# One step of a hybrid recurrent decoder on one core: sample-row outputs and the S5 input matrix on four column groups, modulation in 512-column matmuls

## The chip, the core and the metric

The kernel runs on one core of one Trainium2 chip. The metric is the device time of one execution in microseconds (us); the time of a kernel is the median of its runs.

## What is computed

Two layers of a decoder trunk of width 1024 act on a prompt (512 tokens) and on eight sample rows (one token each, with recurrent states of their own). Per layer:

```python
mod = silu(c) @ w_ada[l] + b_ada[l]            # (9 rows, 6 x 1024): shift, scale, gate, twice
h   = x * (1 + sc_m) + sh_m
out = mixer(h)                                 # layer 0: GLA and RG-LRU; layer 1: S5 and HGRN2
x   = layer_norm(ALPHA * x + (1 + gt_m) * out)
h   = x * (1 + sc_f) + sh_f
x   = layer_norm(ALPHA * x + (1 + gt_f) * swiglu(h, ffn_w_in[l], ffn_w_out[l]))
# GLA and HGRN2, each sample row b and head h, one token:
S[b,h] = diag(a[b,h]) S[b,h] + k[b,h]^T v[b,h]   # (64 x 128 in GLA, 128 x 128 in HGRN2)
o[b,h] = q[b,h] S[b,h]                           # one row of 128
# S5, each of 32 groups g: the response matrix of an 8-token block is made of C_g A_g^e B_g, e = 0..7
```

All arrays are float32. `c` holds nine rows: one for the prompt, eight for the samples.

## The kernel before, in words

Activations lie with features on the 128 partitions and tokens along the free dimension, in two halves of 260 columns (256 prompt tokens and 4 sample rows). A projection is done in units of 128 output features. Each unit splits its weights into a high and a low float32r part (ScalarE casts at L199, VectorE subtracts through the helper at L110) and runs three matmuls per 128 inputs and half: high times high (L237), high times low (L239), low times high (L241). The first units behind a layer norm run one half after the other (L816 to L818). These matmuls of 260 columns are most of TensorE's work.

All weights come through one stream: the list `plan` fixes the order of the pieces, mostly 1 MB each, `WS.load` (L176) issues their loads on SyncE's queue into three buffers, and `WS.take` hands them out in the same order. The pieces of the modulation weights `w_ada` stand in that list between the projections' pieces, placed by `mix`. `WS.ada`, called before and after a unit, takes the modulation pieces that are next. The order of instructions on each engine is chosen when the program is made, by a scheduler that keeps its own estimate of when each operand is ready and otherwise follows the order of the program.

Three places matter here.

- **Modulation.** The first two of layer 0's six parts are made at the start (`ada_mm`, L312). The other ten parts of 1024 columns are made from 40 pieces, four for a part: a piece is 256 rows by 1024 columns of `w_ada`. `ada_part` (L323) runs 8 matmuls for it, two of 128 rows for each of four column groups of the array, with the 32-column `condT` as the stationary operand and 256 columns of weights moving. After the fourth piece `ada_rows` copies the result (ScalarE, L328), turns it with two transposes (L147) and adds the bias on VectorE. The plan places 12 pieces in layer 0's mixer, 8 and 8 in the two halves of its FFN, 8 in layer 1's input projection and 4 at the start of layer 1's FFN.
- **Sample rows.** `la_samples` goes in steps of four rows and one group of heads: 4 steps in GLA (two heads of 64 rows each on the partitions, `hpt` = 2), 8 in HGRN2 (`hpt` = 1). A step makes the outer products with one matmul (L1066, 32 or 64 rows of the array), updates four states on VectorE (L122), multiplies each by its query (L1073: the 128x128 state is the stationary operand, one or two query columns move), copies the result (L1074) and stores the states.
- **S5 input matrix.** `s5_prep` works through four chunks of 8 groups inside layer 0's FFN. Each chunk transposes `BA`, and then multiplies each group's 128x128 `BA` (stationary) by 16 columns of `CS` (L1620), and copies the 128 columns to `Mall` (L1622).

A float32 matmul stands in the trace as two instructions (passes), a float32r matmul as one.

Of the kernel before, what the change touches and what calls it, by code (L numbers as in the profile page):

```python
# [16 lines left out]
D = 1024  # L17
# [22 lines left out]
def build(tc, I, O):  # L40
    nc = tc.nc
    V, S, G, T, SY = nc.vector, nc.scalar, nc.gpsimd, nc.tensor, nc.sync
    with ExitStack() as ctx:
# [65 lines left out]
        def tt(out, a, b, op):  # L109
            V.tensor_tensor(out=out, in0=a, in1=b, op=op)  # L110
# [41 lines left out]
        class WS:  # L152
# [60 lines left out]
            def ada(self):  # L213
                while self.i < len(units) and plan[units[self.i][0]][0] == "ada":
                    p_, _, r = self.take()
                    if p_[2] == 0:
                        self.acc = mx()
                    ada_part(self.acc, p_[2], r)
                    if p_[2] == 6:
                        ada_rows(self.acc, p_[6], p_[4] // 128)  # L220

            def get(self, kind, c0, k0=0, j=0):
# [23 lines left out]
        f_out = [I["ffn_w_out"][l] for l in range(2)]  # L246

        def p_ada(l, js):
            return [("ada", I["w_ada"][l], k0, 2, D * j, D, l) for j in js for k0 in range(0, 8, 2)]

        def p_cols(kind, src, cols):
            return [(kind, src, 0, 8, c, 256) for c in cols]
# [13 lines left out]
        def mix(main, ada, first=1, per=2):  # L266
            r = list(main[:first])
            rest = main[first:]
            done = 0
            for n, c in enumerate(rest):  # L270
                want = (n + 1) * (len(ada) // per) // len(rest) * per
                r += ada[done:want]
                done = want
                r.append(c)
            return r

        FA = p_ada(0, [5]) + p_ada(1, [0])
        FB = p_ada(1, [1, 2])
        OA = p_ada(1, [3, 4])
        LA = p_ada(1, [5])  # L280
        plan.append(("lr", ev_in, 0, 8, 1536, 16))
        plan += p_cols("in", ev_in, [0])
        plan += mix(p_cols("in", ev_in, EV_COLS), p_ada(0, range(2, 4)))
        plan += mix(p_cols("out", ev_out, (0, 256)), p_ada(0, [4])[:2], 1) + p_ada(0, [4])[2:] + p_cols("out", ev_out, (512, 768))
        plan += mix(p_ffn(0, 0)[:12], FA[:4], 3) + mix(p_ffn(0, 0)[12:], FA[4:])
        plan += mix(p_ffn(0, 1)[:-4], FB, 2) + p_ffn(0, 1)[-4:]
        plan += mix(p_cols("in", od_in, OD_COLS), OA, 0, 1)
        plan.append(("glu", I["od_s5_w_glu"][0], 0, 4, 0, 512))
        plan += p_cols("out", od_out, range(0, D, 256))
        plan += mix(p_ffn(1, 0)[:12], LA, 2, 1) + p_ffn(1, 0)[12:] + p_ffn(1, 1)  # L290

        for n, p in enumerate(plan):
            for jj in range(1 if p[0] == "ada" else max(1, p[5] // 128)):
# [15 lines left out]
        def ada_mm(p, r):  # L309
            for k in range(8):  # L310
                c = k % 4
                T.matmul(p[32 * c:32 * c + 32, 0:256], condT[:, k, :], r[:, k, :],  # L312
                         start=(k < 4), stop=(k >= 4), tile_position=(0, 32 * c), skip_group_check=True)
            sb = cst.tile([128, 256], F32, tag="adasb", name="adasb")
            S.copy(sb, p[:, 0:256])
            for b in range(2):
                T.matmul(p[:, 256 + 16 * b:256 + 16 * b + 9], sb[:, 128 * b:128 * b + 128], sel, start=True, stop=True)
            return p[:, 256:288].rearrange("p (c r) -> p c r", r=16)[:, :, 0:9]

        def ada_part(p, k0, r):  # L320
            for k in range(2):
                for c in range(4):
                    T.matmul(p[32 * c:32 * c + 32, 0:256], condT[:, k0 + k, :], r[:, k, 256 * c:256 * c + 256],  # L323
                             start=(k0 + k == 0), stop=(k0 + k == 7), tile_position=(0, 32 * c), skip_group_check=True)

        def ada_rows(p, l, j):
            sb = cst.tile([128, 256], F32, tag="adasb", name="adasb")
            S.copy(sb, p[:, 0:256])  # L328
            for b in range(2):
                transpose(p[:, 256 + 128 * b:384 + 128 * b], sb[:, 128 * b:128 * b + 128])  # L330
            tt(mod[l][:, j:j + 8, :].rearrange("p (c b) r -> p b c r", b=2),
               p[:, 256:512].rearrange("p (b c r) -> p b c r", b=2, r=32)[:, :, :, 0:9],
               bc(vA[:, 48 * l + j:48 * l + j + 8].rearrange("p (c b) -> p b c", b=2).unsqueeze(3), [128, 2, 4, 9]), ALU.add)

        def split(hi, lo, src):
            last["split"] = S.copy(hi, src)
# [678 lines left out]
        def la_samples(mp_, vds, nt, dk, q_s, k_s, a_s, v_s, s_in, s_out, res):  # L1015
# [42 lines left out]
            for bh in range(2):  # L1058
                vd = vds()
                tt(vd.bitcast(F32R), bc(vT.unsqueeze(1), [128, 4, 128]), bc(m8[:, 4 * bh:4 * bh + 4].unsqueeze(2), [128, 4, 128]), ALU.mult)  # L1060
                for t_ in range(nt):
# [376 lines left out]
        def s5_prep(sp):  # L1438
            if True:
# [160 lines left out]
                for ch in range(4):  # L1600
# [417 lines left out]
```

## Time and profile before

| | |
|---|---|
| median of 3 runs (1388.51 to 1391.63) | 1388.89 us |
| the profiled execution's own time | 1391.37 us |
| its span, first to last instruction | 1389.4 us |
| mean granted TensorE clock | 0.985 |
| matmuls busy, share of the span | 96% |
| VectorE, ScalarE, GpSimd busy | 55%, 36%, 14% |
| bytes moved by DMA | 185.53 MB, mean 134 GB/s |

A busy matmul row says that a matmul was in flight; matmuls overlap, so what one costs is read from the starts of the instructions around it, and not from its duration.

### The profile page before, as it was taken

Reading aid. Unit: us, or ns where it says so; the run is one execution under the profiler, and the core shown is the slowest. Engines: PE = TensorE matmul, PEld = TensorE weight load, DVE = VectorE, ACT = ScalarE, POOL = GpSimd, SP = SyncE. Lnnn points to the kernel's source line nnn. Section 1 sums busy time; section 2 is a strip of 40 time slices with the busy share of each in tenths; the row PEclk is TensorE's granted clock in tenths of the full one; section 3 lists DMA queues with packets and bytes.
Section 4 is the critical chain, followed back from the end, with each engine's and each line's share of the span. In section 5 each row is a group of like instructions: output and inputs, shape, how many; then the busy total and the mean of one; then the engine's idle time right before and its main releaser. Section 6 shows DMA issues by size and latency. Waiting matters only on the chain. (4 is left out here: it accounts for less than half of the span.)

```text
span 1389.4 us, 29467 instructions
## 1 busy us (share of the span) xinstructions
PE 1333.4 (96%) x12687; PEld 1267.0 (91%) x12687; DVE 764.9 (55%) x1726; ACT 498.2 (36%) x802; POOL 191.8 (14%) x215
## 2 busy tenths in 40 slices
PE   6998999989999999999998999999999999999996
PEld 4797988989998999999988999889899999999996
DVE  4677755687997233233592785566833233232365
ACT  3555536353232222222264123363533222222231
POOL 2200010340011200000170421013500000000013
PEclk9999999999999999999999999999999999999998
DMA  9643363413345842444458446432333323221211
GB/s 277 197 152 101 91 212 120 154 48 120 116 166 205 234 152 92 152 133 158 150 200 169 131 147 216 126 126 92 101 113 107 118 95 122 92 92 54 84 62 63
DMA packets 157628, 185.53 MB, mean 134 GB/s; under 512 B 18188, under 2 KB 137354, under 8 KB 157242
## 3 DMA queue, kind: packets, MB, share of 16 engines
q1 hardware_dynamic: 151514, 166.43, 38.7%
q0 software_dynamic: 5744, 17.08, 3.8%
q8 instruction: 100, 1.64, 0.5%
q14 instruction: 30, 0.25, 0.1%
q10 hardware_dynamic: 240, 0.13, 0.0%
HBM read 167.11 MB, written 15.36 MB: 131 GB/s over the span
## 5 line engine op out<-in xcount | busy, mean ns | idle before, releaser
L237 PE MATMUL acc<-hhi,whi 128*128 128x260 f32 x1936 | 398.8, 287 | 3.0 <-ACT whi L199 1.3
L199 ACT CAST whi<-raw 128x1024 fp32r<-128x1024 f32 (+2 forms) x198 | 187.7, 955 | 587.1 <-PE acc L239 428.1
L239 PE MATMUL acc<-hlo,whi 128*128 128x260 f32 x1936 | 396.2, 286 | 1.2 <-DVE hlo L110 1.2
L241 PE MATMUL acc<-hhi,wlo 128*128 128x260 f32 x1936 | 395.1, 285 | 0.0
L110 DVE TENSOR_TENSOR wlo<-raw,whi 128x1024 fp32r<-128x1024 f32 (+2 forms) x198 | 220.2, 1116 | 222.3 <-ACT whi L199 220.7
L237 PEld LDWEIGHTS acc<-hhi,whi 128*128 128x128 f32 x1936 | 300.5, 190 | 16.1 <-issue 5.9
L239 PEld LDWEIGHTS acc<-hlo,whi 128*128 128x128 f32 x1936 | 300.6, 190 | 4.4 <-DVE hlo L110 1.7
L241 PEld LDWEIGHTS acc<-hhi,wlo 128*128 128x128 f32 x1936 | 300.9, 190 | 2.3 <-issue 1.7
L239 PE MATMUL acc<-al,whi 128*128 128x260 f32 x576 | 116.0, 283 | 2.3 <-DVE al L110 2.3
L237 PE MATMUL acc<-ah,whi 128*128 128x260 f32 x576 | 116.4, 284 | 1.4 <-DVE x L122 0.8
L241 PE MATMUL acc<-ah,wlo 128*128 128x260 f32 x576 | 115.7, 283 | 0.0
L110 DVE TENSOR_TENSOR sg<-acc,sg 128x520 f32<-128x520 f32 (+1 forms) x48 | 31.0, 653 | 112.6 <-PE acc L241 108.1
L237 PEld LDWEIGHTS acc<-ah,whi 128*128 128x128 f32 x576 | 88.3, 188 | 4.8 <-ACT whi L199 2.3
L239 PEld LDWEIGHTS acc<-al,whi 128*128 128x128 f32 x576 | 88.6, 188 | 2.5 <-DVE al L110 2.5
L241 PEld LDWEIGHTS acc<-ah,wlo 128*128 128x128 f32 x576 | 88.6, 188 | 0.0
L524 POOL TENSOR_TENSOR s<-x 128x520 f32<-128x520 f32 x4 | 6.9, 1720 | 568.1 <-ACT whi L199 321.6
L110 DVE TENSOR_TENSOR smp<-acc,gt 128x8 f32<-128x8 f32 (+1 forms) x72 | 11.6, 161 | 119.0 <-PE acc L241 94.5
L816 PE MATMUL acc<-hhi,whi 128*128 128x260 f32 x208 | 59.2, 287 | 3.3 <-ACT hhi L774 3.3
L818 PE MATMUL acc<-hlo,whi 128*128 128x260 f32 x208 | 58.8, 289 | 3.3 <-DVE hlo L767 1.9
L817 PE MATMUL acc<-hhi,wlo 128*128 128x260 f32 x208 | 58.3, 282 | 0.0
L122 DVE SCALAR_TENSOR_TENSOR x<-acc,gt,x 128x512 f32<-128x512 f32 (+1 forms) x72 | 44.8, 622 | 0.0
L323 PE MATMUL mx<-raw,condT 128*32 128x256 f32 x640 | 44.2, 384 | 0.0
(592 smaller groups left out, 2017.5 us busy)
## 6 DMA issues: line engine op xcount, KB each, us to landing
raw<-in_w_ada_dram SPq DMA_DIRECT2D x40, 1024.0 KB, 6.1
raw<-in_ffn_w_in_dram SPq DMA_DIRECT2D x40, 1024.0 KB, 5.2
raw<-in_ffn_w_out_dram SPq DMA_DIRECT2D x16, 1024.0 KB, 5.3
raw<-in_ev_w_in_dram SPq DMA_DIRECT2D x10, 1024.0 KB, 9.4
raw<-in_od_w_in_dram SPq DMA_DIRECT2D x10, 1024.0 KB, 5.9
raw<-in_w_ada_dram SPq DMA_DIRECT2D x16, 512.0 KB, 7.3
raw<-in_ffn_w_out_dram SPq DMA_DIRECT2D x16, 384.0 KB, 3.1
raw<-in_ev_w_out_dram SPq DMA_DIRECT2D x4, 1024.0 KB, 5.3
```

The lines of the kernel that those rows point to most:

```text
L110: V.tensor_tensor(out=out, in0=a, in1=b, op=op)
L122: V.scalar_tensor_tensor(out=out, in0=a, scalar=s, in1=b, op0=op0, op1=op1)
L199: S.copy(hi[:, :nk, :m], rj)
L237: T.matmul(acc[:, hf, :HN], wh[:, k - koff, :], ah(k)[:, hf, :], start=st, stop=False)
L239: T.matmul(acc[:, hf, :HN], wh[:, k - koff, :], al(k)[:, hf, :], start=False, stop=False)
L241: T.matmul(acc[:, hf, :HN], wl[:, k - koff, :], ah(k)[:, hf, :], start=False, stop=sp)
L323: T.matmul(p[32 * c:32 * c + 32, 0:256], condT[:, k0 + k, :], r[:, k, 256 * c:256 * c + 256], start=(k0 + k == 0), stop=(k0 + k == 7), til ...
L524: G.tensor_tensor(out=lnt["s1"], in0=x[:, 0] if m == 1 else lnt["s1"], in1=x[:, m], op=ALU.add)
L816: T.matmul(out, wh[:, k, :], ah(k)[:, hf, :], start=n == 0, stop=False)
L817: T.matmul(out, wl[:, k, :], ah(k)[:, hf, :], start=False, stop=False)
L818: T.matmul(out, wh[:, k, :], al(k)[:, hf, :], start=False, stop=n == len(ks) - 1)
```

## The change

Three edits, and a new placement of the modulation pieces that follows from the third.

1. In `la_samples` the query becomes the stationary operand, broadcast over the 32 columns of one column group, and the state's 128 columns move. The four rows of a step go to the four column groups. The result, with a row on each group of 32 partitions, is copied by ScalarE and transposed, once for each head of the step.
2. In `s5_prep` two groups' `CS` (32 columns) become the stationary operand and `BA`'s 128 columns move; eight matmuls fill the four column groups twice. Each computes a neighbour's product too. The result is copied, transposed in two blocks, and the wanted halves are copied to `Mall` by two strided copies.
3. A modulation piece is now 128 rows by 2048 columns, and a column group takes 512 moving columns. Eight pieces make two parts. The result fills a whole PSUM bank, so the transposes (four, for two parts) go to a second one.

```diff
-                    if p_[2] == 6:
+                    if p_[2] == 7:
                         ada_rows(self.acc, p_[6], p_[4] // 128)
...
-            return [("ada", I["w_ada"][l], k0, 2, D * j, D, l) for j in js for k0 in range(0, 8, 2)]
+            return [("ada", I["w_ada"][l], k, 1, D * j, 2 * D, l) for j in js for k in range(8)]
...
-        FA = p_ada(0, [5]) + p_ada(1, [0])
-        FB = p_ada(1, [1, 2])
-        OA = p_ada(1, [3, 4])
-        LA = p_ada(1, [5])
+        E2, E4 = p_ada(0, [2]), p_ada(0, [4])
+        FA, FB, OA = p_ada(1, [0]), p_ada(1, [2]), p_ada(1, [4])
...
-        plan += mix(p_cols("in", ev_in, EV_COLS), p_ada(0, range(2, 4)))
-        plan += mix(p_cols("out", ev_out, (0, 256)), p_ada(0, [4])[:2], 1) + p_ada(0, [4])[2:] + p_cols("out", ev_out, (512, 768))
+        plan += mix(p_cols("in", ev_in, EV_COLS), E2 + E4[:4])
+        plan += mix(p_cols("out", ev_out, (0, 256)), E4[4:6], 1) + E4[6:] + p_cols("out", ev_out, (512, 768))
...
-        plan += mix(p_ffn(1, 0)[:12], LA, 2, 1) + p_ffn(1, 0)[12:] + p_ffn(1, 1)
+        plan += p_ffn(1, 0) + p_ffn(1, 1)
...
-        def ada_part(p, k0, r):
-            for k in range(2):
-                for c in range(4):
-                    T.matmul(p[32 * c:32 * c + 32, 0:256], condT[:, k0 + k, :], r[:, k, 256 * c:256 * c + 256],
-                             start=(k0 + k == 0), stop=(k0 + k == 7), tile_position=(0, 32 * c), skip_group_check=True)
+        def ada_part(p, k, r):
+            for c in range(4):
+                T.matmul(p[32 * c:32 * c + 32, 0:512], condT[:, k, :], r[:, 0, 512 * c:512 * c + 512],
+                         start=(k == 0), stop=(k == 7), tile_position=(0, 32 * c), skip_group_check=True)
 
         def ada_rows(p, l, j):
-            sb = cst.tile([128, 256], F32, tag="adasb", name="adasb")
-            S.copy(sb, p[:, 0:256])
-            for b in range(2):
-                transpose(p[:, 256 + 128 * b:384 + 128 * b], sb[:, 128 * b:128 * b + 128])
...
+            sb = tmp.tile([128, 512], F32, tag="t2k", name="adarow")
+            S.copy(sb, p)
+            q = mx()
+            for b in range(4):
+                transpose(q[:, 128 * b:128 * b + 128], sb[:, 128 * b:128 * b + 128])
...
-                    for b in range(4):
-                        T.matmul(po[:, b * hpt:b * hpt + hpt], s0[:, b], qm[:, t_, 4 * bh + b], start=True, stop=True)
-                    V.tensor_copy(o_s[:, t_ * hpt:(t_ + 1) * hpt, 4 * bh:4 * bh + 4], po[:, 0:4 * hpt].rearrange("p (b h) -> p h b", h=hpt))
+                    for hh in range(hpt):
+                        for b in range(4):
+                            T.matmul(po[32 * b:32 * b + 32, 128 * hh:128 * hh + 128], bc(qm[:, t_, 4 * bh + b, hh:hh + 1], [128, 32]),
+                                     s0[:, b], start=hh == 0, stop=True, tile_position=(0, 32 * b), skip_group_check=True)
+                    ot = mp_.tile([128, hpt * 128], F32, tag="ot", name="ot")
+                    S.copy(ot, po[:, 0:128 * hpt])
+                    for hh in range(hpt):
+                        transpose(po[:, 256 + 128 * hh:384 + 128 * hh], ot[:, 128 * hh:128 * hh + 128])
+                    V.tensor_copy(o_s[:, t_ * hpt:(t_ + 1) * hpt, 4 * bh:4 * bh + 4],
+                                  po[:, 256:256 + 128 * hpt].rearrange("p (h b n) -> p h b n", h=hpt, n=32)[:, :, :, 0])
...
-                        gg = 8 * ch + g
-                        T.matmul(pM[:, g * 16:(g + 1) * 16], BA[:, g].rearrange("p e h -> p (e h)"), CS[:, gg],
-                                 start=True, stop=True)
-                    S.copy(Mall[:, 128 * ch:128 * ch + 128], pM[:, 0:128])
+                        c, gg = g % 4, 8 * ch + g - g % 2
+                        T.matmul(pM[32 * c:32 * c + 32, 128 * (g // 4):128 * (g // 4) + 128],
+                                 CS[:, gg:gg + 2].rearrange("p a b -> p (a b)"), BA[:, g].rearrange("p e h -> p (e h)"),
+                                 start=g < 4, stop=True, tile_position=(0, 32 * c), skip_group_check=True)
+                    mt = tmp.tile([128, 256], F32, tag="t2k", name="mt")
+                    S.copy(mt, pM[:, 0:256])
+                    for q in range(2):
+                        transpose(pM[:, 256 + 128 * q:384 + 128 * q], mt[:, 128 * q:128 * q + 128])
...
+                    for b in range(2):
+                        S.copy(mv[:, :, b], pM[:, 256:512].rearrange("p (a b d h) -> p a b d h", b=2, d=2, h=16)[:, :, b, b])
```

With the new pieces the plan places 16 in layer 0's mixer (12 before), 8 and 8 in the halves of its FFN as before, 8 in layer 1's input projection as before, and none in layer 1's FFN (4 before). The pieces are still 1 MB, 40 in all.

## Rows read from the trace of the kernel before

**Rows 1.** The page's first part: busy time of each engine, its share of the span, and its instructions.
```profile
PE 1333.4 (96%) x12687; PEld 1267.0 (91%) x12687; DVE 764.9 (55%) x1726; ACT 498.2 (36%) x802; POOL 191.8 (14%) x215
```
**Rows 2.** Who TensorE waited for: total us, times, longest us. The longest of 27 lines, and one more that the text speaks of.
```profile
PE mx L1716 <- DMA u<-Usd: 5.9, 1, 5.9
...
PE mx L1224 <- issue: 2.8, 1, 2.8
```
**Rows 3.** Groups of TensorE's instructions, shapes kept apart (of L1073 the shape of HGRN2's steps): line, operation, output<-inputs, shapes, count | busy us, mean ns of one | idle before.
```profile
L323 PE MATMUL mx<-raw,condT 128*32 128x256 f32 x640 | 44.2, 384 | 0.0
L1073 PE MATMUL mx<-qm,s 128*128 128x1 f32 x64 | 9.0, 240 | 1.0 <-DVE s L122 0.8
L1620 PE MATMUL mx<-CS,BA 128*128 128x16 f32 x64 | 7.4, 257 | 0.0
```
**Rows 4.** TensorE's timeline around one chunk's S5 products: start us, us, line, shapes, count of merged instructions.
```profile
391.80 0.41 PE L239 MATMUL acc<-hlo,whi 128*128 128x260 f32 x2
392.05 1.85 PE L1620 MATMUL mx<-CS,BA 128*128 128x16 f32 x16
393.75 0.48 PE L241 MATMUL acc<-hhi,wlo 128*128 128x260 f32 x2
394.08 0.40 PE L237 MATMUL acc<-hhi,whi 128*128 128x260 f32 x2
```
**Rows 5.** The same view at the sample rows' products. L1073 stands in 28 runs for 12 steps; these are the first run (GLA) and the last step (HGRN2), which stands in two.
```profile
176.27 0.72 PE L1073 MATMUL mx<-qm,s 128*128 128x2 f32 x6
...
912.07 0.28 PE L241 MATMUL acc<-y5h,wlo 128*128 128x260 f32 x1
912.18 0.50 PE L1073 MATMUL mx<-qm,s 128*128 128x1 f32 x4
912.55 0.37 PE L241 MATMUL acc<-y5h,wlo 128*128 128x260 f32 x1
912.75 0.50 PE L1073 MATMUL mx<-qm,s 128*128 128x1 f32 x4
913.12 0.49 PE L237 MATMUL acc<-y5h,whi 128*128 128x260 f32 x2
913.45 0.28 PE L239 MATMUL acc<-y5l,whi 128*128 128x260 f32 x1
```
**Rows 6.** The same view around two modulation pieces run together, and around one piece alone.
```profile
368.95 0.40 PE L241 MATMUL acc<-hhi,wlo 128*128 128x260 f32 x2
369.28 1.93 PE L323 MATMUL mx<-raw,condT 128*32 128x256 f32 x32
371.14 0.51 PE L237 MATMUL acc<-hhi,whi 128*128 128x260 f32 x2
371.49 0.40 PE L239 MATMUL acc<-hlo,whi 128*128 128x260 f32 x2
...
451.75 1.07 PE L323 MATMUL mx<-raw,condT 128*32 128x256 f32 x16
452.75 0.51 PE L237 MATMUL acc<-ah,whi 128*128 128x260 f32 x2
```
**Rows 7.** The same view: 128 passes of 32 columns on four column groups, and two passes of 512 columns on the whole array.
```profile
845.57 1.30 PE L924 MATMUL mx<-Qs,U 128*32 128x32 f32 x128
846.80 0.44 PE L1832 MATMUL mx<-u,kt 128*128 128x73 f32 x2
...
219.13 0.28 PE L239 MATMUL acc<-hlo,whi 128*128 128x260 f32 x1
219.25 1.02 PE L1008 MATMUL mx<-sqo,ones_ln 128*128 128x512 f32 x2
219.71 0.69 PE L239 MATMUL acc<-hlo,whi 128*128 128x260 f32 x1
220.23 0.40 PE L241 MATMUL acc<-hhi,wlo 128*128 128x260 f32 x2
```
**Rows 8.** The same view around the two transposes of one part of the modulation.
```profile
492.85 0.28 PE L241 MATMUL acc<-ah,wlo 128*128 128x260 f32 x1
492.97 0.38 PE L147 MATMUL mx<-ident,adasb 128*128 128x128 f32 x2
493.11 0.36 PE L241 MATMUL acc<-ah,wlo 128*128 128x260 f32 x1
493.31 0.40 PE L237 MATMUL acc<-ah,whi 128*128 128x260 f32 x2
493.55 0.40 PE L239 MATMUL acc<-al,whi 128*128 128x260 f32 x2
```
**Rows 9.** VectorE's timeline: the four state updates of one GLA step.
```profile
173.39 1.12 DVE L122 SCALAR_TENSOR_TENSOR s<-s,a_s,mx 128x128 f32<-128x128 f32 x4 [1.85 <-PE mx L1066]
```
**Rows 10.** TensorE's timeline: a pair of modulation pieces (32 passes) that fell into two runs, of 12 and 20 passes; the first of them and the instruction behind it.
```profile
239.29 1.06 PE L323 MATMUL mx<-raw,condT 128*32 128x256 f32 x12
240.27 0.50 PE L237 MATMUL acc<-hhi,whi 128*128 128x260 f32 x2
```
**Rows 11.** The same view at the first modulation piece of layer 1's FFN: the matmul that follows its last passes (which start at 992.50), with its wait.
```profile
994.14 0.39 PE L816 MATMUL acc<-hhi,wxh 128*128 128x260 f32 x1 [1.00 <-ACT sg L78]
```
**Rows 12.** ScalarE: its longest wait (total us, times, longest), and the copies of the modulation (ns min/median/max).
```profile
ACT whi L199 <- PE acc L239: 428.1, 117, 6.3
...
L328 ACT COPY adasb<-mx x10: 358/370/374, 122.8 to 1107.7; 128x256 f32<-128x256 f32 x10
```

More of the change, by code (lines that the diff above doesn't have):

```diff
@@ L313, in ada_mm @@
                          start=(k < 4), stop=(k >= 4), tile_position=(0, 32 * c), skip_group_check=True)
-            sb = cst.tile([128, 256], F32, tag="adasb", name="adasb")
+            sb = tmp.tile([128, 256], F32, tag="t2k", name="adasb")
             S.copy(sb, p[:, 0:256])
@@ L318, in ada_mm @@
             return p[:, 256:288].rearrange("p (c r) -> p c r", r=16)[:, :, 0:9]
-        def ada_part(p, k0, r):
-            for k in range(2):
-                for c in range(4):
-                    T.matmul(p[32 * c:32 * c + 32, 0:256], condT[:, k0 + k, :], r[:, k, 256 * c:256 * c + 256],
-                             start=(k0 + k == 0), stop=(k0 + k == 7), tile_position=(0, 32 * c), skip_group_check=True)
-        def ada_rows(p, l, j):
-            sb = cst.tile([128, 256], F32, tag="adasb", name="adasb")
-            S.copy(sb, p[:, 0:256])
-            for b in range(2):
-                transpose(p[:, 256 + 128 * b:384 + 128 * b], sb[:, 128 * b:128 * b + 128])
-            tt(mod[l][:, j:j + 8, :].rearrange("p (c b) r -> p b c r", b=2),
-               p[:, 256:512].rearrange("p (b c r) -> p b c r", b=2, r=32)[:, :, :, 0:9],
-               bc(vA[:, 48 * l + j:48 * l + j + 8].rearrange("p (c b) -> p b c", b=2).unsqueeze(3), [128, 2, 4, 9]), ALU.add)
+        def ada_part(p, k, r):
+            for c in range(4):
+                T.matmul(p[32 * c:32 * c + 32, 0:512], condT[:, k, :], r[:, 0, 512 * c:512 * c + 512],
+                         start=(k == 0), stop=(k == 7), tile_position=(0, 32 * c), skip_group_check=True)
+        def ada_rows(p, l, j):
+            sb = tmp.tile([128, 512], F32, tag="t2k", name="adarow")
[3 more added lines that the diff above has]
+                transpose(q[:, 128 * b:128 * b + 128], sb[:, 128 * b:128 * b + 128])
+            tt(mod[l][:, j:j + 16, :].rearrange("p (c b) r -> p b c r", b=4),
+               q.rearrange("p (b c r) -> p b c r", b=4, r=32)[:, :, :, 0:9],
+               bc(vA[:, 48 * l + j:48 * l + j + 16].rearrange("p (c b) -> p b c", b=4).unsqueeze(3), [128, 4, 4, 9]), ALU.add)
         def split(hi, lo, src):
@@ L1618, in s5_prep @@
                     for g in range(8):
-                        gg = 8 * ch + g
-                        T.matmul(pM[:, g * 16:(g + 1) * 16], BA[:, g].rearrange("p e h -> p (e h)"), CS[:, gg],
-                                 start=True, stop=True)
-                    S.copy(Mall[:, 128 * ch:128 * ch + 128], pM[:, 0:128])
+                        c, gg = g % 4, 8 * ch + g - g % 2
[6 more added lines that the diff above has]
+                        transpose(pM[:, 256 + 128 * q:384 + 128 * q], mt[:, 128 * q:128 * q + 128])
+                    mv = Mall[:, 128 * ch:128 * ch + 128].rearrange("p (a b h) -> p a b h", b=2, h=16)
+                    for b in range(2):
+                        S.copy(mv[:, :, b], pM[:, 256:512].rearrange("p (a b d h) -> p a b d h", b=2, d=2, h=16)[:, :, b, b])
                     yield
```

## The prediction

> **What bounds the kernel.** I read the page's first part first: a matmul is in flight for 96% of the span, the next engine, VectorE, is busy for 55% [rows 1]. Then the waits of TensorE: the longest is one of 5.9 us, and the one of 2.8 us has no releaser that the profile shows [rows 2]. So time is what TensorE's instructions take in their queue, one behind the other; what other engines do costs nothing as long as TensorE has something else to run. The busy sums of the groups [rows 3] are no prices, because matmuls overlap. I therefore price each kind by the timeline: I take the starts of the dense 260-column matmuls on both sides and subtract these at their own pace, 0.24 us for two (493.31 to 493.55, [rows 8]). What is left is what the inserted instructions cost.
>
> - S5 product, 16 passes: 391.80 to 394.08 is 2.28 us, less four dense matmuls (0.48) 1.80, so 0.1125 us a pass [rows 4].
> - Sample product: 912.07 to 913.45 is 1.38 us, less 0.48, 0.90 for 8 passes, again 0.1125 [rows 5]. One moving column costs as much as 16: the pass is paid by the 128x128 stationary operand.
> - Column groups: 16 passes more make a modulation run 0.86 us longer (1.86 against 1.00), which is four rounds of four concurrent passes, 0.215 us a round of 256 columns. The long run inserts 2.54 - 0.48 = 2.06 us; eight rounds are 1.72, so 0.34 us are paid once for each run, for entering and leaving the column groups [rows 6].
> - A transpose: 492.85 to 493.31, less two dense matmuls, is 0.22 for two, 0.11 each [rows 8].
>
> **Two prices the trace doesn't show.** A round of 128 columns lies between one of 32 (1.23 us less 0.34, over 32 rounds: 0.028, [rows 7]) and one of 256 (0.215). On the line between them it is 0.108, which I take; the ends are too far apart to be likelier. A round of 512 is 0.429 on the same line, and two 512-column passes on the whole array insert 1.10 - 0.24 = 0.86, 0.43 each [rows 7]; its bounds are 0.40 and 0.45. Broadcast query columns as stationary operand: I take them like the modulation's 32 columns, which rounds of 0.028 show to be hidden.
>
> **Part by part.** *S5 input matrix.* Out go 4 x 16 passes, 7.2 us. In come, for each chunk, four rounds (0.43), one entry (0.34) and two transposes (0.22): 0.99, 4.0 in all. Gain 3.2 us, if each chunk's 16 passes stay one run, as they do now [rows 4]. It lies inside a dense FFN stage, so it counts fully. ScalarE gets one copy and two short ones more for each chunk, some 1 us by the 0.37 us copy [rows 12]; ScalarE is 36% busy, so I price it at nothing. Without that cover it would be some 3 us.
>
> *Sample rows.* Out go 12 steps of 8 passes, 10.8 us. A whole new step costs 0.34 + 2 x 0.108 + 0.11 = 0.67 in HGRN2, and 0.34 + 4 x 0.108 + 0.22 = 0.99 in GLA, which has two heads and so twice the rounds: 8 x 0.67 + 4 x 0.99 = 9.3. Whole, the change gains 1.5, and in GLA alone it loses. But the steps do not stand whole now: 12 steps stand in 28 runs [rows 5]. The scheduler puts a product into the queue when it thinks that the state is ready, and the four states come from VectorE some 0.28 us apart (1.12 us for four, [rows 9]). Before, such a cut was free. Now every run pays 0.34, and half-filled rounds on top, up to 0.22 in HGRN2 and 0.43 in GLA. If all 16 extra cuts stay (10 in HGRN2, 6 in GLA), that is 5.6 + 4.6 = 10.2 us, 0.64 a cut. The bounds are none and all; I take 7. A new product holds the queue longer than the old one, so the next state is more often ready when the scheduler looks, but the updates stay where they are. That is 4.5 us: the sample rows lose 3.0 net (from -1.5 to +8.7).
>
> *Modulation.* The moving columns stay the same: 80 rounds of 0.429 for 160 of 0.215, -0.1 us. The transposes stay 20. The number of runs changes with the plan: four single pieces leave layer 1's FFN and two pairs join layer 0's mixer, so two entries fewer, -0.7. Unknown is how often a piece is cut. A run of 12 passes took 0.98 us to the next instruction, as long as one of 16 [rows 10]: a cut in the middle of four concurrent passes costs two rounds and an entry, 0.77 now and 1.2 with 512 columns. Three cuts more or fewer are -2.3 to +3.6; I take none. The first piece that leaves the FFN stood ahead of a 1.00 us wait for ScalarE [rows 11]; with it gone, up to that much may come back as a longer wait. The bank for the transposes makes one more PSUM tile wanted for the length of four transposes: I price that at nothing, as the dense units use other banks. SyncE's queue has as many pieces of the same size; four come some 900 us earlier, in a stage where I see no TensorE wait for a weight load [rows 2].
>
> *New waits.* Sixteen times TensorE now waits for a ScalarE copy before a transpose (12 `ot`, 4 `mt`). The copies stand in ScalarE's queue with the weight casts, and these wait for TensorE to free a buffer, 117 times, 428 us in all [rows 12]. Behind a late transpose every dense matmul waits. The modulation has had the same pattern ten times and no wait of TensorE for that copy is among the rows, so I take 0.3 us; bounds 0 and 8 (half of the sixteen a whole microsecond late).
>
> Sum: -3.2 + 3.0 - 0.8 + 0.3 = -0.7 us. The profiled execution took 1391.4 us; it stands 2.5 above the median of the runs, 1388.9. By the sum it would take 1390.7, and the median 1388.2. I say 1388.
>
> **A rule against this change.** Narrow products are priced here by rows 4 and 5 at 0.1125 us a pass. The Trainium skill, TensorEngine Tiling (Array Packing), section Instruction Overhead, says that a matmul has about 60 cycles of overhead, so that one column costs as much as 60, and that no tiling should be taken from a dimension that is already small; an estimate from that page is 25 ns for a pass of the old products, and then only 4 us instead of 18 would be there to save, and the change would cost 13 us. The two rows, with durations for this very thing, speak against it.
>
> **Rivals.**
> 1. *Whole runs.* The scheduler leaves each sample step in one run. -3.2 - 1.5 - 0.8 = -5.5: 1383. For it: wide products; chunks of S5 stand whole now. Against it: 28 runs for 12 steps. Each cut costs 0.64, so it takes at most two cuts to be over 0.3% faster.
> 2. *Cuts stay (slower).* All 16 cuts in `la_samples` remain: -3.2 + 8.7 - 0.8 + 0.3 = +5.0: 1394, and 1395 with one cut wide pair. The change breaks even at 8 cuts; from 15 on it is slower by over 0.3%. For it: VectorE's updates and their pace do not change.
> 3. *Late copies (slower).* Eight transposes a microsecond late: +7.3: 1396. Against it: no such wait for the modulation's copy.
> 4. *Narrow passes were cheap (slower).* If the old 160 passes cost only what the shortest rounds do, 0.028 us [rows 7], 13.5 us less are saved than I count: 1402. This is the mechanism of the page's rule above. Rows 4 and 5 leave it 2 in 100.
> 5. *Moved stalls.* A new order of instructions can add or drop a wait such as the 2.8 us one [rows 2], in either direction; that is in the range and shifts no chance.
>
> **Numbers.** A measurement of this kernel can tell about 0.3%, 4.2 us, from no change. Forecast (some cuts stay, 1384.7 to 1393) 0.53; rival 1 0.26; rival 2 0.14; rival 3 0.05; rival 4 0.02. So faster 0.26, same 0.53, slower 0.21. The range of 8 in 10 takes in rival 1 and most of rival 2: 1382 to 1395.
>
> **What would show it.** In the changed kernel the S5 products should stand in four runs of about 0.8 us and not 1.8, and a modulation run of a pair should be as long as now (2.06 inserted). The new sample products should stand in some 19 runs; their number times 0.34 is what decides. I am wrong in the price if a run of column groups with 128 columns costs other than 0.55 for two rounds; wrong in the mechanism if TensorE waits for `ot`, `mt` or `adarow` copies, or if waits of another stage (the S5 loads, code) differ by more than 3 us.

## The result, and the profile after

The changed kernel takes 1405.88 us (median of 4 runs, 1401.22 to 1408.64) against 1389.38 for the kernel before: ratio 1.0113 [1.0081, 1.0145], slower by some 15.7 us. Measured once more, it is 1405.18 against 1391.66: 1.0102 [1.0084, 1.0121]. The forecast was 1388, no difference, 1382 to 1395.

The page of the changed kernel's profiled execution (1408.64 us, span 1406.9), its first part:
```profile
span 1406.9 us, 28951 instructions
PE 1341.6 (95%) x12423; PEld 1256.5 (89%) x12423; DVE 764.5 (54%) x1721; ACT 502.3 (36%) x817; POOL 192.8 (14%) x215
```
Beside [rows 1] TensorE has 264 fewer instructions and yet is busy for 8.2 us more, and stands still for 65.3 us where it was 56.0. The two belong together. The mean granted clock of the span is 0.977, before 0.985: 32.4 us (1406.9 times 0.023) are lost to the lower level of TensorE's clock, 1.2 instead of 2.4 GHz, before 20.8. The Trainium skill, TensorE: Matmul & The Clock Gate, section Terms, prices time at the low level in this way, as the time times what the clock lacks. In the rows below, dense matmuls at 0.50 start 0.22 us apart (1013.82 to 1014.04), at 1.00 0.12 (402.51 to 402.75 for two).

So I read each kernel by two numbers, each the median over its executions: (1 - granted clock) times span, **lost at half clock**, and what is left of the span, **the rest**. Before (73 executions): 20.9 and 1368.3. After (10): 27.4 and 1375.8. Of the 14 us or so, 6.5 are lost at half clock and 7.5 are in the rest. Neither number is sharp: the clock is recorded to 0.001, which is 1.4 us of a span, and the first also counts time in which TensorE would have waited anyway.

Within a trace the split is better. Each profiled span is made of TensorE's idle time, of what it loses at half clock while it is busy, and of its busy time brought to full clock. Before, these are 56.0, 14.0 and 1319.4. In the changed kernel's two profiled executions the idle time is 9.3 and 8.0 us more, the loss at half clock 9.3 and 7.3 more, and the busy time at full clock 1.1 and 0.5 less.

**The new operations, taken together, do not cost it.** I added up what each run of them puts between its neighbours, as the forecast did, over all runs behind the first 60 us, brought to full clock:

| | before | after | difference | forecast |
|---|---|---|---|---|
| S5 products, with their transposes | 7.1 (4 runs) | 3.7 (4) | -3.4 | -3.2 |
| sample rows' products, with their transposes | 11.1 (28 runs) | 15.3 (31) | +4.1 | +3.0 |
| modulation, with its transposes | 50.6 (35 runs) | 47.0 (30) | -3.6 | -0.8 |

Many of the sample products stand beside narrow work, and what that is taken to cost moves the second line by some 1 us. The sum, a gain of some 3 us, and the 0.5 to 1.1 above agree in that the work does not grow.

The timeline of the changed kernel at an S5 chunk, which answers to [rows 4], and at its transposes:
```profile
402.51 0.40 PE L241 MATMUL acc<-hhi,wlo 128*128 128x260 f32 x2
402.75 0.41 PE L237 MATMUL acc<-hhi,whi 128*128 128x260 f32 x2
403.08 0.65 PE L1625 MATMUL mx<-BA,CS 128*32 128x128 f32 x16
403.66 0.51 PE L239 MATMUL acc<-hlo,whi 128*128 128x260 f32 x2
404.00 0.41 PE L241 MATMUL acc<-hhi,wlo 128*128 128x260 f32 x2
...
406.42 0.28 PE L237 MATMUL acc<-hhi,whi 128*128 128x260 f32 x1
406.54 0.38 PE L147 MATMUL mx<-ident,mt 128*128 128x128 f32 x2
406.67 0.37 PE L237 MATMUL acc<-hhi,whi 128*128 128x260 f32 x1
```
402.75 to 404.00 is 1.25; less four dense matmuls (0.48) that leaves 0.77, against 1.80 before. At a cut sample step (HGRN2, [rows 5]):
```profile
869.67 0.51 PE L239 MATMUL acc<-hlo,whi 128*128 128x260 f32 x2
870.11 0.41 PE L1072 MATMUL mx<-s,qm 128*32 128x128 f32 x2
870.45 0.51 PE L241 MATMUL acc<-hhi,wlo 128*128 128x260 f32 x2
870.79 0.40 PE L237 MATMUL acc<-hhi,whi 128*128 128x260 f32 x2
```
One product of the four (two passes) stands alone. 870.11 to 870.79 is 0.68; less two dense matmuls (0.24) that leaves 0.44. The entry ahead of such a run is 0.09 (402.75 to 403.08 above is 0.33 for two dense matmuls). Together 0.53, for a quarter of the work of a run that the forecast put at 0.55. At a pair of modulation pieces in one run, and at one in three ([rows 6, 10]):
```profile
380.17 0.40 PE L241 MATMUL acc<-hhi,wlo 128*128 128x260 f32 x2
380.50 1.92 PE L320 MATMUL mx<-raw,condT 128*32 128x512 f32 x16
382.35 0.50 PE L237 MATMUL acc<-hhi,whi 128*128 128x260 f32 x2
...
233.22 1.04 PE L320 MATMUL mx<-raw,condT 128*32 128x512 f32 x2
234.20 0.51 PE L237 MATMUL acc<-hhi,whi 128*128 128x260 f32 x2
234.63 1.06 PE L320 MATMUL mx<-raw,condT 128*32 128x512 f32 x8
235.63 0.50 PE L239 MATMUL acc<-hlo,whi 128*128 128x260 f32 x2
235.97 0.40 PE L241 MATMUL acc<-hhi,wlo 128*128 128x260 f32 x2
236.30 1.06 PE L320 MATMUL mx<-raw,condT 128*32 128x512 f32 x6
```
Whole, it is as long as before; in three, each part takes 0.98 to 1.00, two passes as long as eight.

**What costs is standing still.** TensorE's waits in the changed kernel (total, times, longest):
```profile
PE mx L1728 <- DMA u<-Ud: 6.5, 1, 6.5
...
PE mx L468 <- DVE h L110: 4.3, 2, 2.9
PE acc L239 <- DVE al L110: 3.6, 1, 3.6
PE acc L814 <- ACT sg L78: 3.5, 2, 2.4
...
PE mx L922 <- issue: 2.9, 1, 2.9
...
PE mx L922 <- DVE X L110: 2.1, 1, 2.1
...
PE mx L147 <- ACT vt L969: 1.9, 1, 1.9
...
PE mx L320 <- DMA raw<-in_w_ada_dram: 1.6, 1, 1.6
...
PE mx L147 <- ACT ot L1075: 0.5, 1, 0.5
```
The same view of before, of which [rows 2] shows two lines:
```profile
PE mx L470 <- DVE h L110: 2.8, 2, 1.4
...
PE acc L239 <- DVE al L110: 2.3, 1, 2.3
...
PE acc L816 <- ACT sg L78: 2.1, 2, 1.1
...
PE mx L924 <- issue: 0.9, 2, 0.7
```
So `h` has 1.5 more, `al` 1.3, the SwiGLU's `sg` 1.4, `vt` 1.1 (0.8 before), `u` 0.6; the narrow matmuls of GLA's chunks and the one behind them waited 3.7 (2.8 and 0.9) and now 5.4, and the wait for a modulation weight in the mixer is new. These seven are 9.3 us; all idle time together grew by as much. Only the last line is a wait on one of the new copies.

The granted clock (the last column but two) right behind three of these waits, in the changed kernel: stretch, its length, busy us of TensorE, its weight loads, VectorE, ScalarE and GpSimd, clock, DMA share, GB/s:
```profile
443.70:450.50 6.80, 6.04 (x28) 6.04 (x28) 4.68 (x6) 1.46 (x2) 0.00 (x0) 0.50 0.25 73
774.80:781.60 6.80, 4.91 (x56) 4.79 (x56) 2.71 (x10) 0.06 (x1) 1.41 (x2) 0.50 0.75 217
1010.80:1013.70 2.90, 0.53 (x4) 0.31 (x4) 2.70 (x9) 2.11 (x7) 1.68 (x3) 1.00 0.00 0
1013.70:1017.10 3.40, 3.40 (x17) 3.40 (x18) 3.40 (x11) 2.96 (x7) 1.95 (x3) 0.50 0.00 0
```
The first stands behind the 3.6 us wait for `al`, the second behind the 6.5 for `u`, the last behind the 2.4 for `sg`, whose own stretch is the third row. This third wait is the one of [rows 11], 1.00 us then and with no half-clock stretch behind it:
```profile
1010.88 0.29 PE L816 MATMUL acc<-hlo,wxh 128*128 128x260 f32 x1
1013.54 0.48 PE L814 MATMUL acc<-hhi,wxh 128*128 128x260 f32 x1 [2.37 <-ACT sg L78]
1013.82 0.42 PE L815 MATMUL acc<-hhi,wxl 128*128 128x260 f32 x1
1014.04 0.42 PE L816 MATMUL acc<-hlo,wxh 128*128 128x260 f32 x1
```
In this execution the wait is therefore paid twice: 1.4 us more of waiting, and then 3.4 us in which the dense matmuls start 0.22 apart.

### The profile page after: what moved, and what is told of

Same layout as the page of the kernel before. It is cut to its first block, busy times and chain, and to the rows that moved or that the text cites. A ratio compares the mean times of both kernels' runs of the same rounds, so it can differ in the third digit from the quotient of the medians.

```text
span 1406.9 us, 28951 instructions
## 1 busy us (share of the span) xinstructions
PE 1341.6 (95%) x12423; PEld 1256.5 (89%) x12423; DVE 764.5 (54%) x1721; ACT 502.3 (36%) x817; POOL 192.8 (14%) x215
## 4 chain that ended last, share of the span: by engine, by line
PE 78%; DVE 9%; DMA 5%; issue 3%; SPq 2%; ACT 1%; POOL 1%; POOLq 0%; DVEq 0%; ACTq 0%
PE acc L237 20%; PE acc L239 20%; PE acc L241 20%; PE acc L814 3%; PE acc L816 3%; PE acc L815 3%; PE mx L320 2%; PE mx L147 2%; DVE x L110 2%; DVE wlo L110 1%; DMA raw<-in_w_ada_dram 1%; SPq L382 1%; PE mx L1072 1%; DMA u<-Ud 1%; PE mx L999 1%
## 5 line engine op out<-in xcount | busy, mean ns | idle before, releaser
L237 PEld LDWEIGHTS acc<-hhi,whi 128*128 128x128 f32 x1936 | 300.9, 190 | 25.1 <-issue 11.9
L320 PE MATMUL mx<-raw,condT 128*32 128x512 f32 x320 | 42.9, 600 | 1.6 <-DMA raw<-in_w_ada_dram 1.6
```

Source lines behind the costliest of these rows:

```text
L237: T.matmul(acc[:, hf, :HN], wh[:, k - koff, :], ah(k)[:, hf, :], start=st, stop=False)
L320: T.matmul(p[32 * c:32 * c + 32, 0:512], condT[:, k, :], r[:, 0, 512 * c:512 * c + 512], start=(k == 0), stop=(k == 7), tile_position=(0, ...
```

## The experiments

Theories on record: A, the cuts of the sample rows carry the loss; B, the place of the modulation pieces; C, any new order of the queue moves waits; D, the sample edit costs however its runs stand; E, the piece that left layer 1's FFN; H, a wait brings a half-clock stretch. All results, in us (before, measured four times beside these kernels: 1390.35 to 1392.06):

| kernel | median | ratio to before | lost at half clock | rest |
|---|---|---|---|---|
| before | 1390 | 1 | 20.9 | 1368.3 |
| changed (both measurements) | 1405.2, 1405.9 | 1.0102, 1.0113 | 27.4 | 1375.8 |
| e1_s5 | 1386.50 | 0.9963 [0.9948, 0.9979] | 20.1 | 1365.0 |
| e2_samples | 1400.77 | 1.0078 [1.0065, 1.0091] | 21.0 | 1377.4 |
| e3_modulation | 1397.03 | 1.0045 [1.0032, 1.0059] | 23.7 | 1371.6 |
| e4_placement | 1398.50 | 1.0060 [1.0047, 1.0072] | 26.5 | 1371.7 |
| e5_hgrn | 1400.10 | 1.0055 [1.0034, 1.0076] | 22.4 | 1375.9 |
| e6_whole | 1401.42 | 1.0072 [1.0054, 1.0089] | 28.7 | 1370.4 |
| e7_control | 1395.88 | 1.0031 [1.0018, 1.0043] | 25.1 | 1369.1 |
| e8_mixer0 | 1392.22 | 1.0017 [0.9999, 1.0034] | 22.2 | 1367.8 |
| e9_ffn1 | 1401.08 | 1.0061 [1.0038, 1.0084] | 27.3 | 1371.5 |
| e13_late_pieces | 1393.12 | 1.0016 [0.9999, 1.0033] | 23.6 | 1369.6 |
| e10_later | 1385.44 | 0.9953 [0.9936, 0.9971] | 20.8 | 1363.3 |
| e11_fill | 1386.16 | 0.9962 [0.9947, 0.9977] | 18.7 | 1366.8 |
| e12_after_later | 1399.03 | 1.0056 [1.0038, 1.0075] | 23.0 | 1373.5 |

### The three edits, each alone

e1_s5 is the kernel before with the change's S5 lines:
```
-                        T.matmul(pM[:, g * 16:(g + 1) * 16], BA[:, g]..., CS[:, gg], ...)
+                        T.matmul(pM[32 * c:32 * c + 32, ...], CS[:, gg:gg + 2]..., BA[:, g]..., tile_position=(0, 32 * c), ...)
...
```


> The S5 edit alone; sample rows and modulation as before. By the runs in the trace of the changed kernel (four unsplit runs, 2.3 us and 0.55 for their transposes, against 6.8) it saves 4.0 us: 1385.4 beside 1389.4, if nothing else moves. Theory A (cuts: the sample rows carry the loss) and theory B (placement: four more modulation pieces in layer 0's mixer carry it) both expect this, 1384 to 1387. Theory C (moved stalls: any change in the order of instructions brings new waits of several us) expects TensorE's gaps to differ by 3 us or more from the kernel before, so a time up to 1394 is possible.

Measured: 3.9 us less by the medians, 3.3 in the rest; its S5 products and transposes are the same 3.7 us as in the changed kernel. The S5 step of the forecast stands.

e2_samples has the change's lines of `la_samples`, and one line more, for room:
```
-            sb = cst.tile([128, 256], F32, tag="adasb", name="adasb")
+            sb = tmp.tile([128, 256], F32, tag="t2k", name="adasb")
```


> The sample-row edit alone, in GLA and HGRN2; S5 and modulation as before, except that the modulation's 256-column row copy lies in the rotating 2k buffers as in the changed kernel (there is no room otherwise). Theory A: nearly all cuts stay (about 30 runs for 12 steps), and this edit alone costs 8 to 14 us: 1397 to 1403. Theory B: it costs the forecast's 3 us: 1390 to 1394, about 19 to 25 runs. Theory C: 1390 to 1405, with the gaps of TensorE 3 us or more above those of before, at places away from the sample products.

Measured: +10.4 by the medians. The products stand in 36 runs, more than before the change, and with their transposes take 18.0 us for 11.1. That is 6.9 of the 9.1 that the rest grew by. The loss is inside theory A's range; whether the cuts are the cause, e6_whole has to say.

e3_modulation has the 512-column pieces and the new plan, e4_placement the new plan with the old pieces:
```
+        E2, E4 = p_ada(0, [2, 3]), p_ada(0, [4, 5])
+        FA, FB, OA = p_ada(1, [0, 1]), p_ada(1, [2, 3]), p_ada(1, [4, 5])
...
-        plan += mix(p_ffn(1, 0)[:12], LA, 2, 1) + p_ffn(1, 0)[12:] + p_ffn(1, 1)
+        plan += p_ffn(1, 0) + p_ffn(1, 1)
```


> The modulation edit alone: 512-column matmuls in pieces of a k-block, the transposes in a bank of their own, and the new plan with four more pieces in layer 0's mixer and none in layer 1's FFN. Theory A: -1 to +2 us, 1388 to 1391. Theory B: +8 to +12 us, 1397 to 1401, already there at the end of layer 0's mixer, with the half-clock stretch of 10 us at about 126 us that the changed kernel shows. Theory C: anything from 1386 to 1398, with new waits of TensorE.

> Only the placement of the modulation pieces as in the changed kernel (16 pieces in layer 0's mixer instead of 12, none in layer 1's FFN); matmuls of 256 columns and all the rest as before. Theory A: no difference that can be told, 1387 to 1391: two runs of column groups more or fewer. Theory B: the loss is here, 1396 to 1400, as in the modulation edit alone; if the modulation edit is slow and this is not, the 512-column form is what costs. Theory C: 1386 to 1398.

Measured: +6.6 and +8.1. The 512-column form costs nothing that can be told; the placement alone carries the loss of this edit, as theory B has it, though neither kernel has more work: by the sums made as above, e4_placement's modulation takes 48.8 us for 50.6. Its idle time is 4 us more, and 5.6 more are lost at half clock.

The three ratios together make +0.86%, 12.0 us, for 14.2 and 15.7 measured. How this divides can't be told. Against all 73 executions of before, the rest adds up (-3.3 + 9.1 + 3.3 = 9.1, measured 7.5) and the half clock doesn't (-0.8 + 0.1 + 2.8 = 2.1, measured 6.5). Against only those executions of before that ran beside each kernel, it is the other way round: the rest makes 4.0 for 9.8, the half clock 6.6 for 5.2.

### Are the cuts what the sample edit costs?

e6_whole is e2_samples with each product made to wait in the queue's plan for the last of the four updates:
```
+                            tc.add_manual_dep(mm_.ins, st_.ins.name, ..., reason="whole run")
```


> The sample-row edit alone, as in e2_samples, with one thing more: every product of a step waits until all four states are updated, so each of the 12 steps stands as one run (4 matmuls in HGRN2, 8 in GLA). Theory A (the cuts cost it): 12 entries instead of some 31 save about 19 times 0.34, and half-filled rounds besides: 8 to 11 us less than e2_samples, 1389 to 1393; by the forecast's own prices (-1.5) 1389. Theory D (the loss of e2_samples is the broadcast operand, the copies and transposes, or the place of the copy buffer, whatever the runs): 1397 to 1401, as e2_samples. Theory C (moved stalls): between the two, with a gap of several us near 125 us that no sample product causes.

e7_control is the kernel before with nothing but the line of the copy's buffer that e2_samples needed, in its two places:
```
+            sb = tmp.tile([128, 256], F32, tag="t2k", name="adasb")
```

> The kernel before with one thing changed: the copy of a modulation row lies in the rotating 2k buffers, as e2_samples and the changed kernel have it. No work is added or removed. Theory A: 1389 to 1391, so that the whole loss of e2_samples belongs to the products. Theory C (the order of instructions alone moves several us, since a buffer shared with others changes what is scheduled when): 1386 to 1396, and what it differs by is to be taken off e2_samples and e6_whole.

Measured: 12 runs instead of 36, products and transposes 8.4 us instead of 18.0, the rest 7.0 us less than e2_samples: in the work theory A is right. And yet 1401.42, no faster, so its forecast of 1389 to 1393 is missed: 7.7 us more are lost at half clock. The timeline of e6_whole shows where:
```profile
898.21 0.50 PE L1066 MATMUL mx<-vd,kT 32*128 32x512 f32 x1
902.92 0.77 PE L237 MATMUL acc<-y5h,whi 128*128 128x260 f32 x2 [4.21 <-DVE y5h L1950]
907.57 0.66 PE L1074 MATMUL mx<-s,qm 128*32 128x128 f32 x8 [3.88 <-issue]
908.16 0.79 PE L1066 MATMUL mx<-vd,kT 32*128 32x512 f32 x1
908.88 0.80 PE L237 MATMUL acc<-y5h,whi 128*128 128x260 f32 x2
```
Here the dense matmuls that used to stand between the cut products had been pulled ahead of them, TensorE ran out of work twice (before, its waits at this place are 1.6 and 0.8), and from 900.9 on the clock was 0.50 for 13.7 us.

The control misses theory A's 1391: +4.3 us by the ratio, with no work added, and nearly all of it at half clock (+4.2; rest +0.8). Sharing a buffer was enough to set instructions in another order and to move the waits; what of this is the order and what the wait for the shared buffer itself was not taken apart. The changed kernel's copies lie in the same buffers. Theory C holds at this size, and a difference of 4 us between two kernels here says nothing of an operation's price.

e5_hgrn is e2_samples with GLA's old products:
```
+                    if hpt == 1:
...
```


> The sample-row edit in HGRN2 alone; GLA has its old products. The copy of the modulation row lies in the rotating buffers, as in e7_control (1395.9), which is what this is to be compared with. Theory A by the forecast's prices (cuts at 0.43 to 0.56): at full clock 3 to 5 us more than the control, and as GLA's four steps cost the rest of the 8.5, GLA would be the dearer one for each step: 1398 to 1401. Rival (the loss is GLA's, with its twice as many rounds, copies of 256 columns and two transposes): 1 us or less over the control, 1395 to 1397.

Measured: the rest is 6.8 us above the control's, of e2_samples' 8.3. HGRN2 carries most of it, with 22 runs for 8 steps. The forecast's bounds had 3.8 for HGRN2 and 5.0 for GLA: GLA, where I saw the dearer steps, comes out as the cheaper one, though what is left for it, 1.5 us between two kernels, is less than the control moved.

### Where the placement costs

e8_mixer0 moves four pieces from layer 0's FFN into its mixer, e9_ffn1 four from layer 1's FFN into layer 0's:
```
e8  -        FA = p_ada(0, [5]) + p_ada(1, [0])
e8  +        FA = p_ada(1, [0])                  (and p_ada(0, [5]) into the mixer)
e9  -        plan += mix(p_ffn(1, 0)[:12], LA, 2, 1) + ...
e9  +        FA = p_ada(0, [5]) + p_ada(1, [0, 1])     (and so on, no LA)
```


> Old modulation matmuls; only four pieces move, from layer 0's FFN into layer 0's mixer (16 pieces there); layer 1's FFN keeps its four. Theory B (placement costs): moved work cancels (4 us out, 4 us in), and what remains is the 5.6 us that e4_placement loses in layer 0's mixer beyond the moved work: 1394 to 1397. Theory E (the loss of e4_placement lies in layer 1, where the four pieces used to fill TensorE's wait for the first SwiGLU output): no difference, 1388 to 1392.

> Old modulation matmuls; only the four pieces of layer 1's FFN move, into layer 0's FFN; layer 0's mixer keeps its 12. Theory E: the wait for the SwiGLU at the head of layer 1's FFN grows from 1.0 to 2.7 us as in e4_placement and brings a half-clock stretch (1.7 to 3.4 us): 1393 to 1396. Theory B: 1389 to 1392, since the wait alone is 1.7. The forecast's own bound for this was 1.0.

Measured: e8_mixer0 can't be told from no change, and stays under the 1394 of theory B; that the four pieces in layer 0's mixer cost by themselves is not shown. e9_ffn1 costs 8.5, more than theory E says; its trace has the longer wait for `sg` (2.5) but also two waits for weight casts of 4.2 and 2.4 us in layer 0's FFN, where the pieces went. It moves two things at once. So e13_late_pieces only shifts the pieces within layer 1's FFN:
```
-        plan += mix(p_ffn(1, 0)[:12], LA, 2, 1) + p_ffn(1, 0)[12:] + p_ffn(1, 1)
+        plan += mix(p_ffn(1, 0)[:12], LA, 6, 1) + p_ffn(1, 0)[12:] + p_ffn(1, 1)
```


> The kernel before; only the four modulation pieces of layer 1's FFN stand later in it (the first some 80 us later), so that none stands ahead of TensorE's wait for the first SwiGLU output any more. Same work, same stage. Theory E (the piece was what filled that wait): the wait grows from 1.0 to 2.7 us and a stretch at half clock of 3.4 to 6.8 us follows it: 1.7 + 1.7 to 3.4, so 1394 to 1396 against 1390.5. Rival (the wait is filled or hidden by other work; the loss of the placement is elsewhere): 1389 to 1392.

Its timeline at the wait of [rows 11]:
```profile
994.35 0.39 PE L816 MATMUL acc<-hhi,wxh 128*128 128x260 f32 x1 [2.52 <-ACT sg L78]
```
The wait grows from 1.00 to 2.52, nearly the 2.7 expected: the first piece had filled it. The price is 2.2 us by the ratio [-0.1, 4.6], which can't be told from none and is under the 1394 expected: there is the 1.5 of the wait, and in this profiled execution no half-clock stretch behind it, where e4_placement had one of 6.8 us. This wait is 2.4 to 2.7 us in seven of the traces, and a stretch stands right behind it in four (e3_modulation, e4_placement and both of the changed kernel) and not in three (e9_ffn1, e12_after_later, e13_late_pieces). That is theory E in its wait, with a price that is not shown; the rest of e4_placement's 8.1 us is spread over its other waits (1.3, 1.2, 0.9 and 1.5 us in layer 0's mixer) and was not taken apart further.

### Does the wait bring the half clock?

e11_fill is e1_s5 with 24 dense matmuls, whose result goes nowhere, right ahead of the first S5 input product, with the calls of the first two groups of these products moved behind them; e10_later instead holds these products back behind 66 more dense matmuls of the kernel's own; e12_after_later does the latter to the changed kernel:
```
e11 +                    fm = T.matmul(fill[:, 0:HN], hhi[:, n % 8, 0, 0:128], hhi[:, n % 8, 0, :], ...)
...
e10 -                s5_in(0, 4)
...
e10                  unit("in", 512, 0, ev_q)
e10 +                last["hold"] = order["mm"]
e10 +                s5_in(0, 4)
```


> S5 edit alone, and 24 extra matmuls of 260 columns, whose result nobody reads, directly ahead of the first S5 input product: 2.9 us of work that fits into the 3.5 us wait for u; all else stands in the same order as in e1_s5. Theory H (the stretch at half clock comes from TensorE standing still before it): the 3.4 to 6.8 us stretch behind this wait vanishes, 1383 to 1385, faster than e1_s5 although there is more work. Rival (the clock falls there for another reason, or the fall costs nothing): 1386 to 1390.

> S5 edit alone (as e1_s5, 1386.5), and the first S5 input products, which wait 3.5 to 5.9 us for the DMA of u while ready dense matmuls stand behind them, are held back in TensorE's queue behind the next gate unit (66 more dense matmuls, 7.9 us). No work is added or removed. Theory H (a wait costs its own length and, behind it, a stretch at half clock): both go, 3.5 to 5.9 and 1.7 to 3.4 us, 1377 to 1381. Rival (the S5 chain is the bound of this stage, so that what starts later ends later, and the wait only moves to the S5 output): 1385 to 1390.

> The changed kernel, with the first S5 input products held back behind the next gate unit as in e10_later; all three edits stay. Its wait for u was 6.5 us and was followed by 6.8 us at half clock. Theory H: 5 to 10 us faster than the changed kernel, 1396 to 1400 against 1406, so that part of its loss was no price of the new operations. Rival (bound by the S5 chain): 1403 to 1408.

> The changed kernel itself once more, so that its time and its share at half clock rest on more than four runs: 1402 to 1408, of which some 28 us are lost at half clock (before: 21) and the rest is 5 to 6 us more than before. If the sum of the three edits alone holds (-3.9, +10.4, +6.6), 1403.

The place in e1_s5, and then in e11_fill:
```profile
755.35 0.40 PE L239 MATMUL acc<-hlo,whi 128*128 128x260 f32 x2
759.24 2.37 PE L1723 MATMUL mx<-u,bt 128*64 128x72 f32 x48 [3.49 <-DMA u<-Usd]
761.54 0.80 PE L241 MATMUL acc<-hhi,wlo 128*128 128x260 f32 x2
762.14 0.64 PE L237 MATMUL acc<-hhi,whi 128*128 128x260 f32 x2
```
```profile
757.98 0.41 PE L241 MATMUL acc<-hhi,wlo 128*128 128x260 f32 x2
758.22 3.04 PE L1752 MATMUL mx<-hhi 128*128 128x260 f32 x24
763.41 1.75 PE L1725 MATMUL mx<-u,bt 128*64 128x72 f32 x48 [2.14 <-DMA u<-Usd]
```
With the filler the wait is shorter and the clock stays at 1.00: the 48 products behind it take 1.75 us instead of 2.37. The mechanism is as theory H says, in one execution of each. The time is not: 1386.16, as e1_s5, in the rival's range and not under 1385. In this execution the load came 4.2 us later (763.41 for 759.24), so that beside 3.0 us of filler 2.1 us of waiting were left.

e10_later took the 3.5 us wait down to 1.2, but a wait for `vt` of 2.2 us and a half-clock stretch came up some 30 us behind it. At 1385.44 it misses theory H's 1377 to 1381 and lies in the rival's range, 1 us better than e1_s5 and not to be told from it. It is the fastest kernel here, 0.47% [0.29, 0.64] faster than before. e12_after_later is the clear case: 1399.03 against 1405.18 for the changed kernel measured beside it (as expected of that one), with no run of the one (1394.38 to 1402.72) as slow as any of the other (1404.07 to 1409.36). The stretch in which the wait was, in its profiled execution (columns as above):
```profile
765.00:785.00 20.00, 18.85 (x212) 18.38 (x211) 10.37 (x30) 6.18 (x10) 2.87 (x4) 1.00 1.15 186
```
The 6.5 us wait is 1.1, and the clock is 1.00 all through; the rest falls by 2.3 to 4 us, the loss at half clock by 4.4. Between the same two waits for `hhi` on either side of layer 1's mixer, the profiled execution takes 269.3 us, for 278.8 and 277.3 in the changed kernel and 270.6 before, so what was won lies there. Six microseconds are won back by moving a wait that is hardly part of the change's loss (5.9 before, 6.5 after): this shows what such a wait is worth, not where the loss came from.

All traces together bear theory H out for this wait. It is 3.5 to 6.6 us long in the 13 traces in which nothing was done about it, and in each a stretch of 3.4 to 10.2 us at 0.50 begins between 4.3 us ahead of its end and 1.0 us behind it; in e10_later, e11_fill and e12_after_later, where it is 1.2 to 2.1 us, there is none. It is no rule for every wait, as that for `sg` shows, and a stretch can come without one: in e8_mixer0 the clock is 0.50 from 208.5 to 215.3 with no wait of TensorE in the 13 us before; what ran in the last 5 of these were modulation passes on column groups, sample products and GLA's products of 64x128 and 128x128.

## Why the prediction was wrong

Its prices held. **S5**: four whole runs, -3.4 where -3.2 was forecast; narrow passes were dear, so rival 4 is refuted by the run of e1_s5. **A round of 128 columns, the entry**: 0.53 for a run of two rounds, forecast 0.55. **Modulation**: a pair inserts 2.06 as before; -3.6 where -0.8 was forecast, since 30 runs are left of 35; for fewer cuts I had allowed -2.3 more, it is -2.8. **Copies**: one wait of 0.5 for `ot`, none for `mt` and `adarow`; rival 3 did not come about.

**Cuts** were mis-sized: I let 7 of 16 stay; all did and three came besides, 31 runs instead of 19. The term came out at +4.1 for +3.0 all the same, as many of the runs stand beside other narrow work and not between two dense matmuls, where I had priced them. I had also taken the old 28 runs for the most that there can be; e2_samples has 36.

**The step that failed is the fifth rival**, moved stalls, "in the range" and without a chance of its own, with new waits at 0.3 us. The work gains 1 to 3 us. The change lost because its new order brought 8 to 9.3 us of idle time, in the slower trace in seven places, of which one was in my text: I bounded the wait for the SwiGLU at 1.0 more, it is 1.4. Where I wrote that no wait for a weight load was to be seen, there is now one of 1.6 us; the control, with the old plan, has one of 1.1 there too, so the plan need not be its cause. The sign that I had named, waits of other stages that differ by more than 3 us, is there, though no single one of them does. And there are more half-clock stretches, seven and eight of them between 60 and 1360 us in its two traces where before has three, 5 to 9 us more of loss, for which the sum had no term, though in the trace of before the stretch behind the 5.9 us wait of [rows 2] has a granted clock of 0.50 too (columns as above):
```profile
764.60:771.40 6.80, 5.42 (x58) 5.30 (x59) 3.08 (x10) 0.00 (x0) 1.42 (x2) 0.50 0.69 203
```
I had read that wait and not what came after it. The control shows that no operation is needed for it: another buffer for one copy costs 4.3 us. For a kernel whose order comes out of a scheduler's plan, moved stalls were no margin on a sum of -0.7 us, but the larger term.

Not settled: which of the edits brings which wait, as the plan of the whole queue differs in each kernel; how much of the longer waits for ScalarE and VectorE (`h`, `al`, `sg`, `vt`) comes from the order alone and how much from the copies added to their queues; and how the loss of the three edits together divides into waits and half clock.

## What to carry to other kernels

Where one engine is busy for 95% and a scheduler orders its queue, an edit worth a few microseconds of work has to be forecast with a term for the waits that a new order brings, both ways, of the size of what a control with no change in work shows, here 4 us. Price a wait with what stands behind it: if the granted clock falls there, the dense work that follows pays again, in some executions and not in others. And before shortening narrow work, ask what it fills: the cut products and the single modulation piece stood in time that TensorE would otherwise have waited.

## What the hardware showed beyond that

A lone product on one column group, two passes, holds up the queue for as long as four concurrent ones (0.53 and some 0.55 us), and two passes of a modulation piece for as long as eight (0.98 and 1.00).

The wait named "issue" among or right behind GLA's narrow matmuls (2.9 us after, 2.8 before, 4.15 in e2_samples, 4.4 in e6_whole) ended 1.4 to 1.5 us after a 16 KB packet of the DMA queue of kind "instruction" had landed, in each of these traces. It looks as though TensorE waits there for its own program, of which 128 small matmuls use up much in 1.3 us; no experiment was made on it.

The same kernel differs from execution to execution by what it loses at half clock: before, 16.6 to 27.9 us over 73 executions. The Trainium skill, TensorE: Matmul & The Clock Gate, section Part 1: The HAM clock gate, puts the loss of getting up to speed at under 1% of a typical kernel's span. The start of this kernel agrees: in the profiled execution of before, two stretches at 0.50 (24.0 to 30.8 and 51.3 to 58.1) cost 6.8 us, 0.5%. The whole loss at half clock, with the stretches in the middle and at the end, is 1.5% before (20.9 of 1389.0) and 2.0% after (27.4 of 1403.4).
